# A decoder layer's MLP on one core: ten instead of eight seven-product pairs in the first half of the down projection

## The chip, the cores and the metric

The kernel runs on one core of one Trainium2 chip. The metric is the device time of one execution in microseconds (us), as the median of several runs. A profile is one execution taken by the hardware profiler; its times count from the first instruction of that execution.

## What is computed

One layer of a decoder, 256 positions by 2048 channels, in float32: a normalised input projection, two kinds of attention side by side, an output projection with a residual, and an MLP. Only the MLP's second matrix product matters here:

```python
h = _rmsnorm(x, norm_mlp_pre[layer])
u = jnp.square(jax.nn.relu(h @ w_up[layer]))          # 256 x 8192
x = x + _rmsnorm(u @ w_down[layer], norm_mlp_post[layer])   # w_down: 8192 x 2048
```

`u @ w_down` is the down projection: 256 rows, a sum over 8192, and 2048 output columns.

## The kernel before, in words

**Splitting.** Every float32 operand is split into a rounded part `hi` and a remainder `lo` (`split`, L303 to L307): ScalarE writes `hi` (L306), VectorE computes `lo = raw - hi` (L307). One product of a 128x128 block of `u` with a 128x512 block of weights is then three matmuls, hi by hi, hi by lo and lo by hi (`three`, L1016, recorded at L296 in `mm`). TensorE loads the 128x128 block of `u` as the stationary operand before each matmul.

**The two halves.** The down projection is worked in two halves of 1024 output columns (c = 0, then c = 1, the loop at L1197). In each, the sum over 8192 runs over 64 k-tiles of 128, taken as 32 pairs kp = 0 to 31. The 256 rows are two blocks of 128 (b) and the 1024 columns two blocks of 512 (n), so that a pair of k-tiles is a product of 2x2 blocks by 2x2 blocks.

**Eight or seven products.** An ordinary pair is eight block products, 24 matmuls into four accumulators `y` (`down_mm`, L1120), from two weight tiles of 128x1024 that are loaded by SyncE's queue into `raw` (five buffers) and split. A pair listed in `DOWN_SEVEN[c]` is done by Strassen and Winograd's scheme with seven block products, 21 matmuls (`seven_products`, L1021), some into `y` and some into four further accumulators `md`, which `close` (L1037) combines after the half's last such pair. For it, four weight tiles are made on the chip: `b11` (half width), `b`, `u` and `t`, all split into hi and lo. The raw weights of both k-tiles come in one 1 MB transfer by GpSimd's queue (`fetch` in `seven`, L346; `load_two`, L374), alternately into `ab_down` and `c` in the first half. VectorE forms `t` and `u` from them by three sums (L361, L365, L366), into one buffer each. The left side is treated likewise: `down_sums` (L386) forms four 128x128 combinations of blocks of `u` on VectorE (L977 to L979), and `down_split` (L396) splits them into a tile `s`, of which there are two buffers (`down_parts`, L392).

**Sharing between the halves.** The combinations of `u` don't depend on the output columns. For pairs that are in both halves' lists (`SHARED`, L118), the first half stores `s` to memory (`keep_s`, L969, by SyncE's queue), and the second half reads it back (`down_back`, L402, by GpSimd's queue) instead of computing it. The split `u` itself is handled in the same manner: in the first half `split_u` (L951) computes `uhi` on ScalarE and `ulo` on VectorE for each group of two pairs (two buffers each), and `keep_u` stores `ulo`; in the second half `ulo` is read back.

**Order.** All instructions are written out by hand; each engine and each queue does its own in that order. `Weights.emit` (L193) writes the splits of the weight tiles ahead of the matmuls that use them: up to six tiles further (`W_AHEAD`), and with eight buffers for hi and lo (`W_BUFS`) tile i waits until TensorE is done with tile i-8. The side jobs of a seven-product pair are hung on tile numbers by `plan_seven` (L406): with `at = max(len(weights.specs) - SUMS_AHEAD, after)` the left sums come two tiles before `at`, the split of `s` one tile before it, and fetch and sums of the weights at it. Here `after` is the number of the tile behind the pair before that was done with seven products. When two such pairs stand two apart (one ordinary pair between them), `at` is the ordinary pair's first tile, so that the left sums stand ahead of the pair before's `u` and the split of `s` ahead of its `t`. The `split_u` of the next group stands behind the first tile of a group's first ordinary pair. The lists are these:

```python
DOWN_SEVEN = ((7, 11, 13, 17, 19, 23, 25, 29), range(3, 28, 2))
SHARED = [k for k in DOWN_SEVEN[0] if k in DOWN_SEVEN[1]]
```

Of the kernel before, what the change touches and what calls it, by code (L numbers as in the profile page):

```python
# [101 lines left out]
def up_steps(first, *groups):  # L102
    steps = [("k", k) for k in first]
    for i, ks in enumerate(groups):
# [9 lines left out]
N_SEVEN = [sum(w == "w" for w, _ in steps) for steps in UP_STEPS]  # L114


DOWN_SEVEN = ((7, 11, 13, 17, 19, 23, 25, 29), range(3, 28, 2))
SHARED = [k for k in DOWN_SEVEN[0] if k in DOWN_SEVEN[1]]  # L118
GT = FF // 512
DOWN_STEPS = [[s for kp in range(2 * GT)  # L120
               for s in ([("w", kp)] if kp in ws else [("k", 2 * kp), ("k", 2 * kp + 1)])] for ws in DOWN_SEVEN]

# [141 lines left out]
def layer(nc, tc, io):  # L264
# [165 lines left out]
    def seven_down(c, kp):  # L430
        def load():

            n = DOWN_SEVEN[c].index(kp)
            raw = dpl["ab"]
# [762 lines left out]
    for c in range(2):  # L1197
# [3 lines left out]
        accs = {(b, n): y[b][2 * c + n] for b, n in PARTS}  # L1201
        ws = DOWN_SEVEN[c]
        for t, (what, k, tiles) in enumerate(wide_d[c]):
# [105 lines left out]
```

## Time and profile before

| what | value |
| --- | --- |
| median of three runs | 1047.4 us (1047.33 to 1047.88) |
| span of the profiled execution | 1045.7 us |
| first half of the down projection, from its first matmul to the last of pair 29 | about 701.7 to 861.4 us |
| mean granted TensorE clock | 0.997 |

The profiled execution's own device time isn't listed apart from its span; the median lies 1.7 us above the span, which is what lies around it (start and end). In the profile PE is TensorE's matmuls, PEld its loads of stationary blocks, DVE VectorE, ACT ScalarE, POOL GpSimd and SP SyncE. "L306" is line 306. A row of the timeline gives start, length, engine, line, operation, what is written and from what, with idle time before it and what ended it in brackets. The chain is the work that ended last, followed back from the end; matmuls in a chain stand with the time that each adds to it. A windows row gives, for each stretch, the length and then the busy time and count of PE, PEld, DVE, ACT and POOL, the granted clock, the DMA engines' share and GB/s.

### The profile page before, as it was taken

How to read it: one execution, taken by the hardware profiler on the slowest of the kernel's cores; microseconds unless marked ns; L12 is line 12 of the kernel's file. 1: busy time of each engine (PE TensorE's matmuls, PEld its weight loads, DVE VectorE, ACT ScalarE, POOL GpSimd, SP SyncE). 2: the span in 40 equal slices, each digit the busy share in tenths (PEclk: the TensorE clock that was granted, in tenths of full speed). 3: DMA queues.
4: the chain of work that ended last, by engine and by line, in shares of the span. 5: the costliest groups of instructions: out<-in, count | busy, mean ns of one | idle time of the engine just before them, and what ended most of it. 6: DMA issues, size and time to landing. Idle time of an engine off the chain costs nothing.

```text
span 1045.7 us, 13378 instructions
## 1 busy us (share of the span) xinstructions
PE 1035.7 (99%) x4837; PEld 863.2 (83%) x4837; DVE 838.7 (80%) x1122; ACT 630.4 (60%) x848; POOL 51.5 (5%) x83
## 2 busy tenths in 40 slices
PE   9999999999999999999999999999999999999996
PEld 6888889888888888888888888888888888888885
DVE  6676536567557669999999999897899978999995
ACT  6674436565545566665765667666567564766661
POOL 0000000000000000000000000000000000111100
PEclk9999999999999999999999999999999999999998
DMA  9975547454447295646657356378778767698952
GB/s 303 370 229 148 140 129 241 146 162 153 150 156 236 92 360 188 216 147 207 202 185 246 121 201 207 113 253 325 274 276 303 265 232 261 238 332 323 356 204 83
DMA packets 79938, 229.33 MB, mean 219 GB/s; under 512 B 6912, under 2 KB 11520, under 8 KB 79488
## 3 DMA queue, kind: packets, MB, share of 16 engines
q1 hardware_dynamic: 64576, 171.47, 48.9%
q0 software_dynamic: 14864, 56.63, 15.2%
q8 instruction: 38, 0.62, 0.3%
q10 hardware_dynamic: 432, 0.37, 0.1%
q14 instruction: 28, 0.23, 0.1%
HBM read 212.72 MB, written 15.73 MB: 218 GB/s over the span
## 4 chain that ended last, share of the span: by engine, by line
PE 97%; DVE 1%; issue 1%; ACT 0%; POOL 0%; DVEq 0%; POOLq 0%; ACTq 0%
PE y L296 25%; PE acc_u L296 24%; PE acc_o L296 8%; PE m L296 7%; PE md L296 5%; PE acc_qk L296 4%; PE acc_v L296 4%; PE acc_ckv L296 2%; PE acc_ukv L296 2%; PE acc_q L296 2%; PE acc_cq L296 2%; PE acc_k L296 2%; PE acc_uq L296 2%; PE rt L300 1%; PE sc_b L296 1%
## 5 line engine op out<-in xcount | busy, mean ns | idle before, releaser
L307 DVE TENSOR_TENSOR lo<-raw,hi 128x1024 fp32r<-128x1024 f32 (+3 forms) x213 | 241.5, 1152 | 89.8 <-ACT hi L306 89.1
L306 ACT ACTIVATE hi<-raw 128x1024 fp32r<-128x1024 f32 (+3 forms) x213 | 209.9, 999 | 73.6 <-PE y L296 16.1
L296 PE MATMUL y<-hi,uhi 128*128 128x512 f32 x370 | 144.4, 390 | 0.0
L296 PE MATMUL y<-hi,ulo 128*128 128x512 f32 x370 | 144.1, 389 | 0.0
L296 PE MATMUL y<-lo,uhi 128*128 128x512 f32 x370 | 144.0, 389 | 0.0
L296 PE MATMUL acc_u<-hi,hT_hi 128*128 128x512 f32 x356 | 141.7, 398 | 0.0
L296 PE MATMUL acc_u<-hi,hT_lo 128*128 128x512 f32 x356 | 139.2, 391 | 0.4 <-DVE hT_lo L307 0.4
L296 PE MATMUL acc_u<-lo,hT_hi 128*128 128x512 f32 x356 | 138.9, 390 | 0.0
L311 DVE SCALAR_TENSOR_TENSOR lo<-raw,gcol,hi 128x1024 fp32r<-128x1024 f32 x74 | 92.5, 1279 | 9.5 <-ACT hi L310 9.5
L310 ACT ACTIVATE hi<-raw,gcol 128x1024 fp32r<-128x1024 f32 x74 | 83.7, 1148 | 25.0 <-DMA raw<-in_w_up 11.7
L296 PEld LDWEIGHTS y<-hi,ulo 128*128 128x128 f32 x370 | 69.5, 188 | 14.4
L296 PEld LDWEIGHTS y<-lo,uhi 128*128 128x128 f32 x370 | 69.5, 188 | 14.3
L296 PEld LDWEIGHTS y<-hi,uhi 128*128 128x128 f32 x370 | 69.5, 188 | 14.2
L296 PEld LDWEIGHTS acc_u<-hi,hT_lo 128*128 128x128 f32 x356 | 66.8, 188 | 14.9 <-DVE hT_lo L307 0.8
L296 PEld LDWEIGHTS acc_u<-lo,hT_hi 128*128 128x128 f32 x356 | 67.0, 188 | 12.8
L296 PEld LDWEIGHTS acc_u<-hi,hT_hi 128*128 128x128 f32 x356 | 67.0, 188 | 12.8
L306 ACT ACTIVATE hi<-u 128x1024 fp32r<-128x1024 f32 (+1 forms) x38 | 37.4, 990 | 49.2 <-DVE u L366 35.4
L307 DVE TENSOR_TENSOR lo<-st_down,hi 128x1024 fp32r<-128x1024 f32 x42 | 50.4, 1220 | 3.0 <-ACT hi L306 2.8
L296 PE MATMUL acc_o<-hi,mixT_hi 128*128 128x512 f32 x128 | 51.8, 405 | 0.0
L306 ACT ACTIVATE hi<-st_down 128x1024 fp32r<-128x1024 f32 x42 | 43.9, 1052 | 12.6 <-PE y L296 9.5
L296 PE MATMUL acc_o<-hi,mixT_lo 128*128 128x512 f32 x128 | 50.2, 392 | 0.0
L296 PE MATMUL acc_o<-lo,mixT_hi 128*128 128x512 f32 x128 | 50.0, 391 | 0.0
(328 smaller groups left out, 2087.7 us busy)
## 6 DMA issues: line engine op xcount, KB each, us to landing
raw<-in_w_down SPq DMA_DIRECT2D x86, 512.0 KB, 5.8
raw<-in_w_up SPq DMA_DIRECT2D x76, 512.0 KB, 4.6
raw<-in_w_in SPq DMA_DIRECT2D x55, 512.0 KB, 4.9
ab<-in_w_up POOLq DMA_DIRECT2D x22, 1024.0 KB, 5.4
raw<-in_w_out SPq DMA_DIRECT2D x32, 512.0 KB, 4.2
ab_down<-in_w_down POOLq DMA_DIRECT2D x11, 1024.0 KB, 7.1
ukeep<-ulo SPq DMA_DIRECT2D x15, 512.0 KB, 7.0
ulo<-ukeep POOLq DMA_DIRECT2D x15, 512.0 KB, 6.2
```

Source lines behind the costliest of these rows:

```text
L296: nc.tensor.matmul(out, a, b, start=start, stop=stop)
L300: nc.tensor.transpose(out, a, ident)
L306: nc.scalar.activation(hi, src, AF.Copy)
L307: nc.vector.tensor_tensor(out=lo, in0=src, in1=hi.bitcast(F32), op=OP.subtract)
L310: nc.scalar.activation(hi, src, AF.Copy, scale=g)
L311: nc.vector.scalar_tensor_tensor(out=lo, in0=src, scalar=g, in1=hi.bitcast(F32), op0=OP.mult, op1=OP.subtract)
```

## The change

The first half's list gets ten pairs instead of eight. Nothing else is edited; `SHARED` and the schedule follow from the list.

```diff
-DOWN_SEVEN = ((7, 11, 13, 17, 19, 23, 25, 29), range(3, 28, 2))
+DOWN_SEVEN = ((7, 10, 13, 15, 17, 19, 21, 23, 25, 29), range(3, 28, 2))
 SHARED = [k for k in DOWN_SEVEN[0] if k in DOWN_SEVEN[1]]
```

Pairs 10, 15 and 21 become seven-product pairs, and pair 11 becomes an ordinary one. The shared pairs were 7, 11, 13, 17, 19, 23 and 25; they become 7, 13, 15, 17, 19, 21, 23 and 25. The second half's list stays at 3, 5, 7 and so on to 27.

## The prediction

> **What bounds the kernel now.** I read the page's busy times and its chain first, then the windows of the two halves of the down projection, then the chain, VectorE's timeline and the waits inside them.
>
> ```profile
> PE 1035.7 (99%) x4837; PEld 863.2 (83%) x4837; DVE 838.7 (80%) x1122; ACT 630.4 (60%) x848; POOL 51.5 (5%) x83
> PE 97%; DVE 1%; issue 1%; ACT 0%; POOL 0%; DVEq 0%; POOLq 0%; ACTq 0%
> 701.72:741.70 39.98, 39.98 (x186) 33.13 (x185) 29.85 (x35) 24.71 (x29) 2.14 (x3) 1.00 0.80 288
> 798.82:830.10 31.28, 31.28 (x140) 25.91 (x139) 28.86 (x34) 19.69 (x22) 1.43 (x2) 1.00 0.81 286
> 893.34:923.97 30.63, 30.63 (x137) 25.39 (x136) 30.25 (x34) 22.50 (x26) 4.82 (x8) 1.00 0.81 291
> ```
>
> TensorE is the chain: 97% of it, and no idle time in these three stretches. But VectorE's mean of 80% hides stages. Before the first seven-product pair it is busy 29.85 of 39.98 us; in six pairs with two of them (798.82 to 830.10) 28.86 of 31.28; in the second half, every second pair, 30.25 of 30.63. TensorE never waits, because VectorE works ahead; it has little left to give.
>
> ```profile
> 741.70 0.68 PE md L296 x3
> ...
> 767.54 5.44 PE y L296 x24
> 772.98 0.68 PE md L296 x3
> ...
> 776.38 1.36 PE md L296 x6
> 777.74 16.32 PE y L296 x72
> ...
> 804.26 0.68 PE md L296 x3
> ```
>
> An ordinary pair takes 5.44 us (24 matmuls, 0.2267 us each). Pair 13, with seven products, runs from 772.98 to 777.74: 4.76 us. So each pair turned over saves 0.68 us of TensorE.
>
> **The change, part by part.** *Removed from TensorE:* two more such pairs in all, six matmuls, 2 x 0.68 = 1.36 us. This is all that the change can give: 0.13%. Pair 13 still starts at 772.98 (two pairs of seven products stand before it, as now).
>
> *Added to VectorE:* its cost is read from one run of its timeline without a break, from the left sums of pair 19 on.
>
> ```profile
> 783.04 0.42 DVE L977 TENSOR_TENSOR st_down<-uT 128x256 f32<-128x256 f32 x1
> 783.49 0.29 DVE L978 TENSOR_TENSOR st_down<-st_down,uT 128x128 f32<-128x128 f32 x1
> 783.82 0.29 DVE L979 TENSOR_TENSOR st_down<-uT,st_down 128x128 f32<-128x128 f32 x1
> 784.03 1.22 DVE L307 TENSOR_TENSOR lo<-st_down,hi 128x1024 fp32r<-128x1024 f32 x1
> 785.16 0.69 DVE L307 TENSOR_TENSOR s<-st_down,s 128x512 fp32r<-128x512 f32 x1
> 785.76 1.22 DVE L307 TENSOR_TENSOR lo<-st_down,hi 128x1024 fp32r<-128x1024 f32 x1
> 787.02 1.22 DVE L361 TENSOR_TENSOR st_down<-ab_down 128x1024 f32<-128x1024 f32 x1
> 788.28 0.69 DVE L365 TENSOR_TENSOR st_down<-st_down,ab_down 128x512 f32<-128x512 f32 x1
> 789.00 0.69 DVE L366 TENSOR_TENSOR st_down<-st_down,ab_down 128x512 f32<-128x512 f32 x1
> 789.62 1.22 DVE L307 TENSOR_TENSOR lo<-raw,hi 128x1024 fp32r<-128x1024 f32 x1
> 790.75 1.22 DVE L307 TENSOR_TENSOR ulo<-uT,uhi 128x1024 fp32r<-128x1024 f32 x1
> 791.89 1.22 DVE L307 TENSOR_TENSOR lo<-raw,hi 128x1024 fp32r<-128x1024 f32 x1
> 793.02 0.69 DVE L307 TENSOR_TENSOR lo<-ab_down,hi 128x512 fp32r<-128x512 f32 x1
> 795.25 1.23 DVE L307 TENSOR_TENSOR lo<-ab_down,hi 128x1024 fp32r<-128x1024 f32 x1 [1.54 <-ACT hi L306]
> ```
>
> From start to start: left sums 0.99, lo of u 1.13, lo of s 0.60, lo of t 1.26, the weights' sums 2.60, first ordinary tile 1.13, ulo 1.14, second ordinary tile 1.13; then lo of b11 0.60 (as long as s) and lo of b 1.14 (as ulo). That is everything for one seven-product pair and one ordinary pair: **11.72 us**. TensorE needs 4.76 + 5.44 = **10.20 us** for the two. In the list before, such a neighbourhood (11 and 13, 17 and 19, 23 and 25) is followed by three ordinary pairs, and VectorE recovers there: six pairs cost it 28.86 of 31.28. In the new list 13 to 25 are six such neighbourhoods in a row. VectorE falls behind by 1.52 us in each, after its lead is used up.
>
> *How long the lead lasts.* The new list adds one wait. `s` has two buffers, so the split of `s` for pair 17 needs the buffer of pair 13, and waits for 13's last matmul; in the first half before, the pair but one behind always stood six pairs away. The present lead there is 19.1 us (lo of s for 19 at 785.16, its pair from 804.26 on), the distance from the end of 13 to the start of 17 only 5.44 + 4.76 + 5.44 = 15.64. The same wait stands in the second half, at pair 27 for the end of pair 23:
>
> ```profile
> 995.37 5.44 PE y L296 x24
> 995.40 0.63 ACT L306 ACTIVATE s<-st_down 128x512 fp32r<-128x512 f32 x1 [2.75 <-PE md L296]
> 996.07 0.69 DVE L307 TENSOR_TENSOR s<-st_down,s 128x512 fp32r<-128x512 f32 x1 [0.98 <-ACT s L306]
> 997.02 1.23 DVE L307 TENSOR_TENSOR lo<-st_down,hi 128x1024 fp32r<-128x1024 f32 x1 [0.26 <-ACT hi L306]
> 998.28 1.23 DVE L361 TENSOR_TENSOR st_down<-ab_down 128x1024 f32<-128x1024 f32 x1
> ```
>
> The pair ends at 995.37; lo of s starts 0.70 later, lo of t 0.95 after that, and then the sums as usual. What stands behind the waiting split on ScalarE is hi of t and of the ordinary tiles; VectorE waits for those. Now the ledger. Pair 13 ends at 772.98 + 4.76 = 777.74, lo of s for 17 starts at 778.44. To lo of s for 19 it is 11.72 + 0.35 (t comes 0.95 instead of 0.60 later): 790.51. By then pair 15 has ended (787.94), so the wait costs nothing any more and VectorE runs without a break: s for 21 at 802.23, for 23 at 813.95, for 25 at 825.67.
>
> Which of its results is late first? Behind lo of s come t, the sums, the first ordinary tile and ulo, which starts 0.60 + 1.26 + 2.60 + 1.13 = 5.59 later and ends 1.22 after that. The ordinary pair that follows begins a new group and needs this ulo in its third matmul, whose stationary load stands 0.07 us behind the pair's start, as in the ordinary pair 14 from 777.74 on:
>
> ```profile
> 777.81 0.19 PEld L296 LDWEIGHTS y<-hi,ulo 128*128 128x128 f32 x1
> ```
>
> With 0.04 us from one engine's end to the other's start (996.03 to 996.07 above), ulo is there 6.85 us after lo of s. Pair 18 starts two cycles behind 777.74, at 798.14, pairs 20, 22 and 24 each 10.20 later. Pair 18: ulo at 797.36, wanted at 798.14 + 0.07 = 798.21, 0.85 early. Pair 20: 809.08 against 808.41, 0.67 late. Pair 22: 820.80 against 818.61, 2.19 late in all. Pair 24: 832.52 against 828.81, **3.71 us** late in all. Behind 25 come three ordinary pairs and VectorE catches up (each costs it 2.26 and half an ulo, under 3, against 5.44), so no more is lost; by pair 29 it is waiting for buffers again and the second half starts as it does now.
>
> *Other pieces of the first half.* The transfers of raw weights carry the same bytes. A fetch waits for lo of b two pairs of the list earlier, some 18 us ahead of its sums, and lands in time:
>
> ```profile
> 783.42 0.71 POOL L374 DMA_DIRECT2D c<-in_w_down  x1 [17.21 <-DVE lo L307]
> c<-in_w_down POOLq DMA_DIRECT2D x4, 1024.0 KB, 8.9
> skeep<-s SPq DMA_DIRECT2D x7, 512.0 KB, 6.8
> ```
>
> One store of `s` more goes past SyncE's queue (eight instead of seven, 6.8 us to landing). It waits for its split, which lies over 12 us ahead of its use, and the raw loads behind it are wanted a cycle later still; I cost it at nothing. If that cover were gone, a raw load would be late by at most those 6.8 us once.
>
> *The second half.* Pair 11 isn't shared any more: its left sums and split return, 0.99 + 0.60 and a few hundredths, say 1.65 us on VectorE, ahead of the ordinary pair 10. Pairs 15 and 21 lose theirs, later.
>
> ```profile
> 920.59 2.35 DVE L307 TENSOR_TENSOR lo<-raw,hi 128x1024 fp32r<-128x1024 f32 x2
> 923.97 5.44 PE y L296 x24
> ```
>
> Pair 10 starts at 923.97 and takes its first lo in its second matmul, at about 924.0; that lo ends now at 920.59 + 1.22 = 921.81, then at 923.46. It stays hidden, with half a microsecond to spare.
>
> *The sum:* -1.36 + 3.71 = +2.35 us. On the profiled execution the span becomes 1048.1; the median stands 1.7 above the span, so 1047.4 + 2.35 = **1049.8 us**. Of the two unknown sizes the cycle matters most: 0.15 us more or less in 11.72 counts four times, 0.6; the start of the ledger may be earlier by up to 1 us if the wait for pair 13 doesn't bind. The forecast's own range is thus 1048.9 to 1050.6.
>
> *A rule on the clock.* In the first microseconds of the trace matmuls run at half the later rate:
>
> ```profile
> 1.19 3.59 PE L521 MATMUL warm<-zero 128*128 128x512 bf16 x8 [1.19 <-DVE zero L518]
> ```
>
> Eight took 3.59 us, 0.45 each, against 0.2267. The Trainium skill ("TensorE: Matmul & The Clock Gate", section "A second HAM failure mode: psum-queue depth-cycling") says that frequent small idle spells between groups of matmuls can make TensorE's clock go back and forth between half and full rate. By that rule the new stalls would cost more than their own length. No run so far shows such a spell in this stage, where the granted clock is 1.00 in each window; I leave it out of the sum and keep it as a rival.
>
> **The rivals.** *No stall (8%):* VectorE's lead covers the deficit, and only TensorE's gain is left: 1047.4 - 1.36 = 1046.0. For it speaks that the second half runs every second pair without a wait; against it, that there ulo and most of s come from memory, and VectorE is still 30.25 of 30.63 busy. It decides if the cycle costs VectorE under about 10.8 us, since 0.6 in each of four cycles is what the lead at pair 16, 0.85 + 1.52 us, would cover. *A smaller stall (16%):* the wait for pair 13 doesn't bind or the cycle is 0.15 shorter, 2.7 to 3.1 late: 1048.9. *The second half stalls too (8%):* the half microsecond at pair 10 isn't there, the whole 1.65 is exposed less 0.5: 1050.9. *Half clock after stalls (3%):* three spells of the 3.59 us seen at the start, each costing half of that, 5.4 us: 1055.2. *The wait costs more than itself (5%):* split of s and store hold up the raw loads once, bounded by 6.8 us; nearest the forecast, 1052. That the change doesn't do what it says I give nothing: the list alone decides which pairs have 21 matmuls.
>
> **How the numbers follow.** The forecast has 60%, 1049.8. The range 1047.8 to 1051.2 leaves out the case without stall below and the clock and queue cases above. About 0.2%, 2.1 us, is what a measurement of this kernel can tell from no change; the forecast stands only just beyond it, at 1049.5. Of its 60%, some 42 lie above; with the second half's, the clock's and the queue's 16, slower has 0.58. Same has 0.41: the rest of the forecast, the smaller stall and the case without. Faster needs over 2.1 us where TensorE gives 1.36: 0.01.
>
> **What would show it.** Right: TensorE has idle time at the starts of pairs 20, 22 and 24, about 0.7, 1.5 and 1.5 us, ended by VectorE's ulo (L307); VectorE is busy without a break from about 779 to 845; ScalarE's split of s for 17 waits for `md` near 777.7; the end of pair 29 lies 2.35 us later than now, and the second half has its present length. Wrong: no idle TensorE there (lead was larger), stalls ended by a transfer (queues), a granted clock under 1.00 behind them, or new idle time near pair 10 of the second half.

## The result and the profile after

The changed kernel takes 1051.13 us (median of 6 runs, 1050.24 to 1051.53) against 1047.45 us (6 runs, 1047.33 to 1047.88): ratio 1.0033, 95% interval 1.0021 to 1.0044. It is slower by about 3.5 us by the ratio, by 3.68 by the medians; 2.35 were forecast.

The page's busy times and its chain by engine, as before:

```profile
PE 1036.3 (99%) x4831; PEld 861.5 (82%) x4831; DVE 848.1 (81%) x1136; ACT 631.1 (60%) x853; POOL 53.1 (5%) x86
PE 90%; DVE 6%; DMA 1%; issue 1%; ACT 0%; POOL 0%; DVEq 0%; POOLq 0%; SPq 0%; ACTq 0%
```

Six matmuls fewer, as counted. The shares of busy time hardly say anything, but the chain does: TensorE fell from 97% to 90% of it, VectorE has 6%, and a transfer 1%. The 6% are the stretch in which VectorE's work sets the pace, not what was lost in it. Where the time went is read from the chain's times. Three marks serve for all kernels: the first matmul of the down projection, the end of pair 29, and the first matmul of the last group (L1188 in the kernel before, a few lines further where an edit adds lines).

| kernel | first mark | first half to the end of pair 29 | from there to the last group |
| --- | --- | --- | --- |
| before | 701.72 | 159.66 | 165.27 |
| after | 701.93 | 162.17 (+2.51) | 165.87 (+0.60) |

The span went from 1045.7 to 1049.2: 2.51 in the first half, 0.60 in the second, and 0.2 each ahead of the first mark and behind the last, where nothing was changed. These rows of the chain of the changed kernel carry the table:

```profile
701.93 4.76 PE y L296 x21
...
864.10 27.20 PE y L296 x120
...
1029.97 5.45 PE y L1188 x24
```

**The first half.** TensorE's waits from 700 to 1030 us (in total, times, longest) come from VectorE in five places and from a transfer in one:

```profile
PE y L296 <- DVE ulo L307: 1.7, 3, 0.6
PE y L296 <- DVE lo L307: 0.7, 2, 0.4
PE y L296 <- DMA ulo<-ukeep: 0.3, 1, 0.3
```

Busy times of matmuls overlap, so such a wait shows smaller than it is; the stationary loads (PEld) give the places in the first half. In brackets stands the idle time ahead of each:

```profile
809.41 0.19 PEld L296 LDWEIGHTS y<-hi,ulo 128*128 128x128 f32 x1 [0.83 <-DVE ulo L307]
...
820.04 0.19 PEld L296 LDWEIGHTS y<-lo,uhi 128*128 128x128 f32 x1 [0.79 <-DVE lo L307]
821.18 0.19 PEld L296 LDWEIGHTS y<-hi,ulo 128*128 128x128 f32 x1 [0.95 <-DVE ulo L307]
...
831.82 0.19 PEld L296 LDWEIGHTS y<-lo,uhi 128*128 128x128 f32 x1 [0.78 <-DVE lo L307]
832.95 0.19 PEld L296 LDWEIGHTS y<-hi,ulo 128*128 128x128 f32 x1 [0.95 <-DVE ulo L307]
```

These are the first tiles of pairs 20, 22 and 24, and each time ulo, the third matmul's operand, is the last to come. Between the loads of an undisturbed pair, too, there are 0.04 us, so the loss is better read from pair to pair: from the first load of pair 20 to that of pair 21 it takes 6.14 us (808.16 to 814.30) instead of 5.44, from 22 to 23 7.02 (819.06 to 826.08), from 24 to 25 7.03 (830.84 to 837.87). That is 0.70, 1.58 and 1.59 us lost, 3.87 in all.

VectorE's timeline shows why. Each row of s here is the lo of the split that opens a cycle of two pairs, for 17, 19, 21, 23 and 25:

```profile
778.65 0.69 DVE L307 TENSOR_TENSOR s<-st_down,s 128x512 fp32r<-128x512 f32 x1 [0.93 <-ACT s L306]
779.60 1.23 DVE L307 TENSOR_TENSOR lo<-st_down,hi 128x1024 fp32r<-128x1024 f32 x1 [0.26 <-ACT hi L306]
...
790.73 0.68 DVE L307 TENSOR_TENSOR s<-st_down,s 128x512 fp32r<-128x512 f32 x1
...
802.50 0.69 DVE L307 TENSOR_TENSOR s<-st_down,s 128x512 fp32r<-128x512 f32 x1
...
814.27 0.69 DVE L307 TENSOR_TENSOR s<-st_down,s 128x512 fp32r<-128x512 f32 x1
...
826.04 0.69 DVE L307 TENSOR_TENSOR s<-st_down,s 128x512 fp32r<-128x512 f32 x1
...
831.68 1.22 DVE L307 TENSOR_TENSOR ulo<-ab,uhi 128x1024 fp32r<-128x1024 f32 x1
```

From 790.73 on the cycles are 11.77 us long, each time, with no idle time in between; TensorE would need 10.20. Only the two rows of the first cycle have a wait, and ScalarE's row says for what: for the last matmul of pair 13, which ends at 773.19 + 4.76 = 777.95.

```profile
777.99 0.63 ACT L306 ACTIVATE s<-st_down 128x512 fp32r<-128x512 f32 x1 [2.69 <-PE md L296]
```

**The second half.** The chain has one piece that wasn't there:

```profile
967.76 0.42 POOL s L404
...
968.30 10.11 DMA ulo<-ukeep
...
978.45 1.66 PE y L296 x6
```

GpSimd's queue issues the read-back of s for pair 21 and behind it the ulo for pair 20. That ulo takes 10.11 us to land, and pair 20's third matmul waits for it. Before, pair 21 wasn't shared, nothing stood ahead of this ulo, and it was issued 1.06 us ahead of the end of pair 17 (964.77) instead of 0.83 behind it:

```profile
963.71 0.55 POOL L960 DMA_DIRECT2D ulo<-ukeep  x1 [7.08 <-PE y L296]
```

### The profile page after: what moved, and what is told of

It is laid out like the page before. It is cut to its first block, busy times and chain, and to the rows that moved or that the text cites. A ratio compares the mean times of both kernels' runs of the same rounds, so it can differ in the third digit from the quotient of the medians.

```text
span 1049.2 us, 13382 instructions
## 1 busy us (share of the span) xinstructions
PE 1036.3 (99%) x4831; PEld 861.5 (82%) x4831; DVE 848.1 (81%) x1136; ACT 631.1 (60%) x853; POOL 53.1 (5%) x86
## 4 chain that ended last, share of the span: by engine, by line
PE 90%; DVE 6%; DMA 1%; issue 1%; ACT 0%; POOL 0%; DVEq 0%; POOLq 0%; SPq 0%; ACTq 0%
PE acc_u L296 24%; PE y L296 21%; PE acc_o L296 8%; PE m L296 7%; PE md L296 4%; PE acc_qk L296 4%; PE acc_v L296 4%; DVE lo L307 3%; PE acc_ckv L296 2%; PE acc_ukv L296 2%; PE acc_q L296 2%; PE acc_cq L296 2%; PE acc_k L296 2%; PE acc_uq L296 2%; PE rt L300 1%
## 5 line engine op out<-in xcount | busy, mean ns | idle before, releaser
L307 DVE TENSOR_TENSOR lo<-raw,hi 128x1024 fp32r<-128x1024 f32 (+3 forms) x209 | 236.7, 1151 | 86.2 <-ACT hi L306 85.6
L306 ACT ACTIVATE hi<-raw 128x1024 fp32r<-128x1024 f32 (+3 forms) x209 | 205.9, 998 | 79.3 <-DMA raw<-in_w_in 18.4
L296 PE MATMUL y<-hi,ulo 128*128 128x512 f32 x358 | 139.8, 390 | 2.0 <-DVE ulo L307 1.7
L296 PE MATMUL y<-lo,uhi 128*128 128x512 f32 x358 | 139.6, 390 | 0.7 <-DVE lo L307 0.7
L296 PE MATMUL y<-hi,uhi 128*128 128x512 f32 x358 | 139.7, 390 | 0.0
L296 PEld LDWEIGHTS y<-hi,ulo 128*128 128x128 f32 x358 | 67.2, 188 | 17.3 <-DVE ulo L307 2.7
L296 PEld LDWEIGHTS y<-lo,uhi 128*128 128x128 f32 x358 | 67.2, 188 | 15.4 <-DVE lo L307 1.6
L296 PEld LDWEIGHTS y<-hi,uhi 128*128 128x128 f32 x358 | 67.2, 188 | 13.8
L307 DVE TENSOR_TENSOR lo<-st_down,hi 128x1024 fp32r<-128x1024 f32 x46 | 55.3, 1221 | 2.6 <-ACT hi L306 2.6
L306 ACT ACTIVATE hi<-st_down 128x1024 fp32r<-128x1024 f32 x46 | 47.6, 1049 | 6.5 <-PE y L296 3.8
```

What stands on the lines that cost most here:

```text
L296: nc.tensor.matmul(out, a, b, start=start, stop=stop)
L306: nc.scalar.activation(hi, src, AF.Copy)
L307: nc.vector.tensor_tensor(out=lo, in0=src, in1=hi.bitcast(F32), op=OP.subtract)
```

## The experiments

The theory after the first look: in the first half VectorE's cycle is too long for TensorE's, and the run of such cycles is longer than VectorE's lead; in the second, the read-back of 21 holds ulo back in a crowd of transfers. The first rival: the wait for the buffer of s makes the stalls. The second: ten pairs are too many, wherever they stand. All compared times are against the kernel before on the same chip (1047.65 to 1047.82 there).

**Without the left sums of pairs 15 to 25 in the first half** (part of the computation is left out):

```diff
-        four_sums(q, uT[kp // 2][:, k:k + 2, :].rearrange("p k s -> p (k s)"))
+        if c or not 15 <= kp <= 25:
+            four_sums(q, uT[kp // 2][:, k:k + 2, :].rearrange("p k s -> p (k s)"))
```

> The changed kernel without the left sums (three VectorE instructions, 0.99 us) of pairs 15 to 25 in the first half; the combinations of an earlier pair are used in their place. Theory (VectorE's work per cycle of two pairs, 11.77 us against TensorE's 10.20, makes the stalls): a cycle takes 10.78, the deficit 0.58 in four cycles stays within the 2.4 us lead at pair 16, no stall in the first half, 1047.45 - 1.36 = 1046.1 us plus up to 0.9 from the second half. Rival (the wait for the buffer of s makes them: VectorE can't start on a pair before the pair but one ahead has ended): the wait stays and so do most of the stalls, 1050 to 1051 us.

1047.27 us, ratio 0.9993 (0.9984 to 1.0002). ScalarE's split of s for 17 still waits for pair 13. Then a window from about pair 13's start over 60 us, with its length and busy times as in the windows before, and the end of pair 29:

```profile
778.12 0.63 ACT L306 ACTIVATE s<-st_down 128x512 fp32r<-128x512 f32 x1 [2.75 <-PE md L296]
```
```profile
772.98:833.00 60.02, 60.02 (x266) 49.70 (x265) 55.80 (x58) 42.00 (x47) 4.29 (x6) 1.00 0.83 284
```
```profile
860.37 27.20 PE y L296 x120
```

TensorE is busy all through. From the first mark (702.07) the first half takes 158.30 us: 159.66 - 1.36 exactly. The stalls of the changed kernel are thus 162.17 - 158.30 = 3.87 us, as counted from the loads, and 0.99 us less VectorE work per cycle removes them all, with the buffer's wait still in the order. The second half lost 1.13 us at pair 20 here (166.40), which hides the gain in the total.

**A third place for the s of pair 17:**

```diff
+        if (c, kp) == (0, 17):
+            st = [late["up"].tile([P, 512], F32R, tag="r", bufs=2, name=f"s17_{w}") for w in range(2)]
+            return st, [[st[w][:, i * P:(i + 1) * P] for w in range(2)] for i in range(4)]
```

with the split and two stores of it to match.

> The changed kernel with a third place for s, used by pair 17 alone (two tiles of 128x512 that are free then), so that 17's split doesn't wait for the end of pair 13, and 19's and 21's find theirs free earlier. Theory (the cycle's work makes the stalls, and the wait only takes VectorE's lead once): VectorE starts its unbroken run about 1.3 us earlier, the first half's stalls go from 3.9 to about 2.5 us, in two places (pairs 22 and 24) instead of three, 1049.7 us. Rival (the wait makes the stalls): they go altogether, 1047.0 us. Third: the wait isn't what took the lead, no difference, 1051.1 us.

1049.63 us, ratio 1.0017 (1.0008 to 1.0026). The split of s for 17 no longer waits for TensorE, and the stalls before ulo are two:

```profile
777.38 0.63 ACT L306 ACTIVATE s<-st_down 128x512 fp32r<-128x512 f32 x1 [1.32 <-DVE st_down L986]
...
820.45 0.19 PEld L296 LDWEIGHTS y<-hi,ulo 128*128 128x128 f32 x1 [0.92 <-DVE ulo L307]
...
832.22 0.19 PEld L296 LDWEIGHTS y<-hi,ulo 128*128 128x128 f32 x1 [0.95 <-DVE ulo L307]
```

The first half (from 702.68 to 863.34) takes 160.66, 2.36 us of stalls instead of 3.87. The wait is worth 1.5 us, once; the rest is the cycle's. The rival that the wait alone makes the stalls falls. The second half takes 165.28 here, with 21 shared: in this profile ulo came just in time, 9.0 us after its issue.

**Eight pairs, standing close:**

```diff
-DOWN_SEVEN = ((7, 11, 13, 17, 19, 23, 25, 29), range(3, 28, 2))
+DOWN_SEVEN = ((7, 13, 15, 17, 19, 21, 23, 25), range(3, 28, 2))
```

> Eight pairs as in the kernel before, but standing close: 7, 13, 15, 17, 19, 21, 23, 25. The same matmuls as before. Theory (density, not number): the run from 13 on is that of the changed kernel, so the same 3.9 us of stalls and no gain on TensorE: 1047.45 + 3.9 = 1051.3 us, plus up to 0.9 from the second half (21 is shared): 1051.3 to 1052.2 us. Rival (more seven-product pairs cost in themselves): as before, 1047.5 us.

1052.43 us, ratio 1.0042 (1.0028 to 1.0056), with no matmul more or fewer than before. A window from the same time on, 65 us long, in which TensorE is busy for only 62.83, and the transfer in the second half's chain:

```profile
772.98:838.20 65.22, 62.83 (x272) 50.56 (x272) 61.34 (x73) 41.08 (x47) 3.58 (x5) 1.00 0.75 249
```
```profile
969.43 10.60 DMA ulo<-ukeep
```

From the first mark to the last group it is 329.90 us against 324.93 before: 4.97 more. The end of pair 29, at 865.22, splits this into 3.86 in the first half, as in the changed kernel, and 1.11 by ulo in the second.

**Nine pairs, without 21:**

```diff
-DOWN_SEVEN = ((7, 11, 13, 17, 19, 23, 25, 29), range(3, 28, 2))
+DOWN_SEVEN = ((7, 10, 13, 15, 17, 19, 23, 25, 29), range(3, 28, 2))
```

> The changed list without pair 21: nine pairs, of which 13, 15, 17 and 19 stand close, then three ordinary pairs. Theory (the lead covers the deficit of 1.57 us per cycle through pair 18, where the prediction's ledger has 0.85 us to spare, and the three ordinary pairs give it back): no stall in the first half, 21 isn't shared so none at pair 20 of the second, 1047.45 - 0.68 = 1046.8 us. Rival (every neighbourhood two apart stalls): two stalls or more, 1048 to 1050 us.

1047.36 us, ratio 0.9997 (0.9989 to 1.0006). First half 158.98 (703.51 to 862.49), 0.68 less than before; second half 165.26. No stall. The total's interval can't tell this gain from none; the two marks can.

**Ten pairs, spread:**

```diff
-DOWN_SEVEN = ((7, 11, 13, 17, 19, 23, 25, 29), range(3, 28, 2))
+DOWN_SEVEN = ((5, 7, 10, 13, 15, 17, 19, 23, 25, 29), range(3, 28, 2))
```

> Ten pairs as in the changed kernel, but begun earlier and with a gap: 5, 7, 10, 13, 15, 17, 19, 23, 25, 29. The same number of matmuls as the changed kernel. Theory (density): VectorE is idle a quarter of the time ahead of pair 7 and has room for pair 5; no stall in the first half, the whole gain of 1.36 us: 1046.1 us, faster than both. Rival (ten pairs are too many for VectorE in this half): stalls as in the changed kernel, 1049 to 1051 us.

1046.72 us, ratio 0.9990 (0.9981 to 0.9999): faster than the changed kernel, and a little faster than the kernel before, with an interval that ends just under 1. Its chain:

```profile
703.04 4.76 PE y L296 x21
...
861.34 27.20 PE y L296 x120
...
1026.58 5.46 PE y L1188 x24
```

158.30 and 165.24 us: the whole 1.36 us of six matmuls and no loss. Ten aren't too many, so the second rival falls. The gain in the total, about 1.0 us, is no larger than what runs differ by.

**Pair 21 not shared:**

```diff
-SHARED = [k for k in DOWN_SEVEN[0] if k in DOWN_SEVEN[1]]
+SHARED = [k for k in DOWN_SEVEN[0] if k in DOWN_SEVEN[1] and k != 21]
```

> The changed kernel, but pair 21 isn't shared: the second half computes its left sums and splits s itself (about 1.65 us more of VectorE there), and GpSimd's queue has no read-back of s for 21 ahead of the ulo for pair 20. Theory (the second half's new stall comes from this read-back: it waits for the end of pair 17 and holds the ulo transfer behind it back by about 4.6 us in the busiest stretch of the transfers): the 0.7 us stall at pair 20 goes, the first half's stalls stay at 3.9 us, the time is 1047.45 - 1.36 + 3.9 = 1050.0 us. Rival (transfers are only slower there, whatever the queue's order): the stall stays, 1050.9 to 1051.1 us. Second rival (VectorE in the second half has no room for the 1.65 us): a new stall ended by VectorE, over 1051 us.

1050.58 us, ratio 1.0027 (1.0017 to 1.0037). First half 162.14, second half 165.24: the stall at pair 20 is gone, and VectorE's added work there costs nothing.

**The loads of x and gains eight k-tiles later:**

```diff
-            if (c, what, k) == (1, "k", 40):
+            if (c, what, k) == (1, "k", 48):
```

> The changed kernel with the second half's loads of x and of the gains (four of 512 KB and two of 256 KB) moved from k-tile 40 to k-tile 48. Theory (the late ulo needs both: the place behind the read-back, and the crowd of transfers): with the crowd gone ulo lands in about 6.5 instead of 10.1 us, no stall at pair 20, 1050.0 us; the crowd may then make a like stall four pairs later, since read-backs stand ahead of ulo there too, and the time would stay at 1050.5 to 1051. Rival (order in the queue alone is enough): the stall at pair 20 stays, 1051 us.

1051.43 us, ratio 1.0034 (1.0021 to 1.0046). The ulo for pair 20, in the same place behind the read-back, now lands after 4.8 us, in time. The stall moves with the crowd, two groups on, to pair 24 behind the read-back for 25:

```profile
988.10 0.42 POOL s L404
...
988.64 10.43 DMA ulo<-ukeep
...
999.11 5.30 PE y L296 x22
```

**The read-backs behind ulo**, all pairs shared as in the changed kernel:

```diff
-        for n, f in (*more, (0, fetch), (-late_sums, sums), *((0, f) for f in last)):
+        for n, f in (*more, (0, fetch), (-late_sums, sums), *((-1, f) for f in last)):
```

> The changed kernel with the second half's read-backs of s written one tile later, so that on GpSimd's queue each stands behind the next group's ulo instead of ahead of it; 21 stays shared, the loads of x and gains stay at k-tile 40. Theory (the late ulo comes from its place behind the read-back, in a crowd that ulo alone just bears): ulo for pair 20 is issued about 1.9 us earlier and lands in time, no stall in the second half, the first half as in the changed kernel: 1047.6 + 2.5 = 1050.1 us, as with 21 not shared. Rival (the additional 512 KB read in the crowd makes it late, in whatever order): the stall of 0.6 to 1.1 us stays, 1050.9 us. Third (s itself comes late now): a stall ended by the read-back.

1050.50 us, ratio 1.0026 (1.0015 to 1.0037). First half 162.11, second half 165.26. GpSimd's queue now has ulo for pair 20 ahead of the read-back:

```profile
966.26 0.55 POOL L960 DMA_DIRECT2D ulo<-ukeep  x1 [7.62 <-PE y L296]
967.61 0.53 POOL L404 DMA_DIRECT2D s<-skeep  x1 [0.81 <-PE md L296]
```

The bytes are the same; the order alone removes the stall. Ulo lands 7.3 us after its issue here. Together the three runs say that it takes both, the place in the queue and the crowd.

**Pair 11 not shared, in the kernel before:**

```diff
-SHARED = [k for k in DOWN_SEVEN[0] if k in DOWN_SEVEN[1]]
+SHARED = [k for k in DOWN_SEVEN[0] if k in DOWN_SEVEN[1] and k != 11]
```

> The kernel before with pair 11 not shared: the second half computes its left sums and split itself. Theory (the 1.65 us of VectorE ahead of pair 10 of the second half are hidden, with half a microsecond to spare): no difference, 1047.45 us. Rival (they aren't hidden, VectorE is at its limit there): up to 1.1 us slower, 1048.5 us.

1047.89 us, ratio 1.0001 (0.9992 to 1.0010). Second half 165.26. The lo for pair 10 starts at 923.00 and pair 10 at 924.74: hidden, with the half microsecond to spare that the prediction had.

**Eleven pairs, spread**, read-backs behind ulo:

```diff
-DOWN_SEVEN = ((7, 11, 13, 17, 19, 23, 25, 29), range(3, 28, 2))
+DOWN_SEVEN = ((5, 7, 9, 11, 15, 17, 19, 23, 25, 27, 29), range(3, 28, 2))
```

> Eleven pairs, never more than four of them two apart in a row: 5, 7, 9, 11, 15, 17, 19, 23, 25, 27, 29, with the read-backs behind ulo as in the run beside it. Theory (what counts is how long VectorE's cycle of 11.77 us runs against TensorE's 10.20 before two ordinary pairs more give the lead back): three or four such cycles stay within the lead, no stall in the first half, 159.66 - 3 x 0.68 = 157.6 us for it, 1047.6 - 2.0 = 1045.6 us, faster than all. Rival (a four-long run without the slack in front uses the lead up, and two ordinary pairs between runs don't give it back): stalls of 0.5 us or more by ulo at pairs 12, 20 or 28, 1046.5 us or more.

1049.24 us (1047.39 to 1052.06), ratio 1.0015 (1.0005 to 1.0024): a miss. The first half is as expected, pair 29 ends at 859.40, 157.63 us from the first mark at 701.77, without a stall. But the second half takes 169.2 us, 4.0 more than without a stall. Its loss is at pair 4, where VectorE's lead is smallest in the kernel before, too (0.2 us, 893.17 against 893.34). TensorE's timeline there, and a window over it:

```profile
891.21 0.51 PE L296 MATMUL y<-hi,uhi 128*128 128x512 f32 x1
893.76 0.79 PE L296 MATMUL y<-lo,uhi 128*128 128x512 f32 x1 [2.04 <-DVE lo L307]
894.35 0.63 PE L296 MATMUL y<-hi,ulo 128*128 128x512 f32 x1
894.78 0.63 PE L296 MATMUL y<-hi,uhi 128*128 128x512 f32 x1
...
897.21 0.39 PE L296 MATMUL y<-hi,uhi 128*128 128x512 f32 x1
897.43 0.39 PE L296 MATMUL y<-lo,uhi 128*128 128x512 f32 x1
```
```profile
892.00:896.00 4.00, 2.24 (x5) 1.82 (x6) 4.00 (x5) 4.00 (x6) 0.18 (x1) 0.70 0.86 279
```

Of the 4.0 us, 2.3 are the wait for lo, and 1.6 the slow matmuls behind it (see the last section). ScalarE had waited for a raw weight tile at the change of halves, and VectorE behind it. The load of this tile had itself been released by a result of VectorE, as the chain shows:

```profile
860.63 1.06 ACT L306 ACTIVATE hi<-raw 128x1024 fp32r<-128x1024 f32 x1 [3.95 <-DMA raw<-in_w_down]
```
```profile
853.60 1.23 DVE lo L307
...
854.84 5.69 DMA raw<-in_w_down
```

Read from this one trace, pairs 25, 27 and 29 in a row leave VectorE without its lead just where the second half needs it. Neither this nor the late load as the cause was tried by itself. The runs of this kernel spread over 4.7 us, so what one profile shows needn't be the loss of each.

## Why the prediction was right, and where it fell short

The median, 1051.13 us, lies just inside the stated range of 1047.8 to 1051.2 and above the forecast's own 1048.9 to 1050.6. The first half came as forecast, in mechanism and nearly in size (2.51 us against 2.35 from mark to mark). The second half's loss isn't in the sum, and that the total still fits in the range is luck: the run with the later loads, where this loss is 0.97 us instead of 0.60, takes 1051.43. Of the signs named beforehand, those of being right came in the first half; one of being wrong, a stall ended by a transfer, came in the second.

*TensorE's gain, 1.36 us:* right to the hundredth, as the two ten-pair kernels without stalls show (158.30 against 159.66).

*VectorE's cycle, 11.72 us:* 11.77 was measured. Three cycles of 0.05 more make nearly all of the 0.16 by which the stalls exceed the ledger (3.87 against 3.71).

*The wait for pair 13 and its timing:* right. ScalarE waited for `md`, and lo of s started 0.70 us behind pair 13's end, as in the row of the second half that was used for it. That the ledger could start up to 1 us earlier without the wait was right too: in the run with a third place, lo of s came 1.0 earlier, counted from the first mark, and lo of t 1.35. With three cycles of 11.72 there, 0.05 shorter each, that makes the 1.5 by which the stalls fell.

*Which result is late, and where:* right. Ulo at pairs 20, 22 and 24, with 0.70, 1.58 and 1.59 us lost where the ledger has 0.67, 1.52 and 1.52; pair 18 had none. What the ledger left out is that lo of the first ordinary tile is late as well at 22 and 24; it adds nothing, since ulo comes after it.

*The return of VectorE's lead by pair 29, and pair 11 in the second half:* right in what follows from it; the second half is as long as before (165.24 to 165.28) wherever ulo is in time. But it was closer than the prediction had it. VectorE was to be busy without a break until about 845; in the changed kernel its first wait comes in pair 29 itself, 15 us later:

```profile
860.47 3.50 DVE L307 TENSOR_TENSOR lo<-raw,hi 128x1024 fp32r<-128x1024 f32 x3 [0.61 <-ACT hi L306]
```

Why it took so much longer wasn't looked into.

*The step that failed:* "Pairs 15 and 21 lose theirs, later", with no cost. It counted what leaves VectorE and not what enters GpSimd's queue. A shared pair's read-back waits for the buffer of s, that is for the end of the pair but one before, and everything behind it on that queue waits with it: ulo, wanted 10.2 us after that end, was issued 1.9 us later than before. (The 4.6 us in one of the expectations compare times on the clock; pair 17 itself ended 2.7 later.) That alone would have left it in time (0.83 + 7.5 = 8.3 us behind the end of pair 17, against 10.2); it also took longer to land. From 970 to 975 us the DMA engines are fully busy, before (share 1.03) as after:

```profile
970.00:975.00 5.00, 5.00 (x23) 4.13 (x22) 4.43 (x5) 2.65 (x3) 0.00 (x0) 1.00 1.03 409
```

In this crowd ulo landed 7.3 to 7.5 us after its issue in the kernel before and in the runs without the read-back or with it behind, and 9.0 to 10.6 us after it behind the read-back. Whether it is the read-back's bytes ahead of it or its later start in the crowd that makes this difference isn't shown. The loss is 0.60 us in the changed kernel's profile, 0.97 to 1.13 in three others and nothing in one. With the first half's 2.51 this makes the 3.1 us between the marks. The rest of the span's 3.5 is 0.2 at each end, where the kernels are the same; in the profiles of all runs the first mark lies between 701.70 and 703.51, and the stretch behind the last mark takes 19.0 to 19.4 us, so both are within what executions differ by.

*The rivals:* a wait in the second half was given 8%, but at pair 10 and by VectorE; a queue's cost was given 5%, but for the stores. Each had the kind of thing right and the place wrong. The clock after stalls stayed at 1.00 in the changed kernel: behind the idle spells of 0.8 to 0.95 us at pairs 22 and 24 the loads stand 0.23 us apart again. So the rule of the Trainium skill ("TensorE: Matmul & The Clock Gate", section "A second HAM failure mode: psum-queue depth-cycling") shows no effect here. What a longer spell did in one run stands in the last section.

## What to carry to other kernels

An engine that works ahead can look nearly idle enough on average and still be too slow in a run of dense stages: compare its work with the bound engine's per repeating unit, and ask how many units the lead lasts. Then the same number of costly units can be had by spreading them, as 5, 7, 10, 13, 15, 17, 19, 23, 25, 29 show against 7, 10, 13, 15 to 25, 29. When work on an engine is replaced by a transfer, go along its queue: what waits in front of what, and how late is the one behind.

## What the runs showed beside this

TensorE's granted clock fell behind one short idle spell. In the run with eleven pairs, 2.04 us without a matmul (2.55 from one start to the next) were followed by some seven matmuls 0.43 us apart instead of 0.2267, until 896.9. The granted clock, 0.70 over the window shown with that run, was 0.50 inside the slow stretch:

```profile
895.00:896.00 1.00, 1.00 (x3) 0.77 (x3) 1.00 (x2) 1.00 (x2) 0.00 (x0) 0.50 0.84 299
```

It is one case. In the changed kernel spells under 1 us, two of them 1.1 us apart, changed nothing.

The start of the down projection, with all code before it the same, lay between 701.70 and 703.51 us in the profiles. Differences of totals under 1 us are therefore better read between marks inside one trace.
